# Order of loads and splits at the head of each layer's passes, and the second layer's first norm factors made in the output projection

## The chip, the cores and the metric

The kernel runs on one core of a Trainium2 chip. The metric is the device time of one execution in microseconds, the median of several runs. The engines named below are TensorE (PE; its weight loads PEld), VectorE (DVE), ScalarE (ACT), GpSimd (POOL) and SyncE (SP), which issues every DMA of this kernel. Each engine works through its own instructions in a fixed order.

## The reference: what is computed

Two layers over 2048 tokens of width 1024, in float32. Each layer normalises x, applies one input projection whose columns are split between two groups of heads, mixes them, and adds the output projection to x:

```
h = rmsnorm(x, norm_g[l]);  z = h @ w_in[l]
g_q, g_k, g_v, g_lr, g_gate, c_q, c_kv, k_pe, m_gate = split(z)
log_a = log_sigmoid(g_lr @ w_gla_gate_up[l] + b_gla_gate[l]) / 16
o_gla = gla_mix(g_q, g_k, g_v, log_a, gla_norm_g[l]) * silu(g_gate)    # chunked gated linear attention
q  = rmsnorm(rmsnorm(c_q) @ w_uq[l]);  k, v = from rmsnorm(c_kv) @ w_ukv[l] and k_pe
o_mla = block_causal_attention(rope(q), rope(k), v) * silu(m_gate)
x = x + concat([o_gla, o_mla]) @ w_out[l]
```

## The kernel before

Tokens are cut into 16 tiles of 128, taken in 8 pairs. To keep float32 accuracy every large product is three matmuls (`mm3`, L98 to L101): both operands are split into a rounded high part (made on ScalarE) and the rest (made on VectorE or GpSimd); high times high, high times low and low times high are summed. `block` (L321) runs such a product over the 8 slices of the width (k = 0 to 7) and, after a slice, calls what a dictionary `ins` holds for it. So "at k = 3" means: these instructions stand in TensorE's order behind slice 3, with four groups of three matmuls of the block done.

Each layer has four stages.

1. `pass1` (L364) computes for each pair of tiles (`pair`, L592) four kinds of block: `mi` (latents, rotary key, low-rank gate input) for tile a and b, then `qk` and `v` for a, then `qk` and `v` for b. x is not normalised ahead of the product; the factor 1/rms of each token is kept in `rt` and applied to the results. Between the slices stand the small steps of linear attention: `gates_a` transposes the low-rank input `lr` that `lat_chain` made with the factor, `gates_b` multiplies it by the gate weights (`lg`), `gates_c` sums the log gates (`bp`), `gla_kv` updates the state (`kv`), `gla_o` makes the output (`op`). `tail(t)` says at which k the last two come.
2. `pass2` (L711) multiplies by the two gate weights (`gt`, `mg`), applies SiLU (`gate_y`, `gate_m`), transposes the gated output tile `on` (`out_t`) and makes the queries from the latent (`queries`, with the weight `w_uq` split into `uq`). It runs in the same pairs.
3. `phase_b` is causal attention, head by head.
4. `phase_c` is the output projection: for each quarter q of the tokens 8 column blocks m, each a product `co` over 8 slices, then `done` adds x. After the first layer `done` also stores the new x (`xd`) and sums its squares over the columns (`ac`, stored as `sd[q]`).

Where the factors come from: in the first layer `norm_load(t)` loads a tile of x (`xn`, one buffer) and `norm_s(t)` squares and sums it on ScalarE, and for two tiles at a time `norm` makes the factors. In the second layer `load_s(q)` loads `sd[q]` (tile `ss`) and `norm_q(q)` sums it over the partitions by four matmuls with a column of ones (each recorded as two), then `norm`. The factors of the first four tiles are made at slice 2 of the very first `mi` block (L599).

The order of work: TensorE runs in program order throughout. In the first pair of each layer ScalarE and VectorE run in program order as well (`BOOT`, in the `with` at the end of `pass1`); there the loads and the splits of the weights are listed by hand, and `boot.update` places some of them by (block, k). Everywhere else, and for SP and GpSimd everywhere, a planner lays down each engine's order at build time from durations that it assumes, among ready instructions in program order. A tile's buffers are shared by tag: in `pass1` and `pass2` the tag "x" has three buffers of 1024 columns, "stg" three staging buffers that weights, `kq`, `vr`, `on`, `qs` and others take in turn. A load into a buffer waits until its last user is done.

The `w_uq` splits: `split_small` (L282) loads 128x384, ScalarE makes the high part and VectorE the low part; there are four of them, written at the start of `pass2.run`.

Of the kernel before, what the change touches and what calls it, by code (L numbers as in the profile page):

```python
# [9 lines left out]
F32 = mybir.dt.float32  # L10
# [3 lines left out]
ALU = mybir.AluOpType  # L14
# [5 lines left out]
P = 128  # L20
# [33 lines left out]
def trunk(ctx: ExitStack, tc: tile.TileContext, x, xT, xt, positions, w_mi, w_qk, w_v, w_gt, w_mg, pk, w3s,  # L54
# [306 lines left out]
        V.tensor_tensor(out=rt[:, t:t + n, 2], in0=r, in1=r, op=ALU.mult)  # L361


    def pass1(l, wp, pp, w1, lat, hT01):  # L364
        sm = smalls[l]

# [17 lines left out]

        def norm_load(t):

            sss[t] = w1.tile([P, D], F32, tag="xn", name="xn", bufs=1)
            dma(sss[t], x[t * P:(t + 1) * P, :])

        def norm_s(t):  # L390
# [9 lines left out]
            dma(sss[q], sd[q])  # L400

        def norm_q(q):
            ps, ss = pp.tile([P, 8], F32, tag="tp", name="tp"), sss.pop(q)
            for i in range(4):
                T.matmul(ps[:, 2 * i:2 * i + 2], lhsT=ss[:, i * P:(i + 1) * P], rhs=ones, start=True, stop=True)
            v = w1.tile([P, 4], F32, tag="xv", name="xv")
            V.tensor_scalar(out=v, in0=ps[:, 0:8:2], scalar1=1.0 / D, scalar2=None, op0=ALU.mult)
            norm(w1, v, 4 * q, 4)

        def lat_chain(t, mi):  # L410
            lt = lr[:, t % 2]
# [162 lines left out]
            dma(od[t], osn)  # L574

        def tail(t):
            return {2: [lambda: gla_kv(t)], 4: [lambda: gla_o(t)]}

        def go(f, *a):
            return lambda: f(*a)  # L580
# [11 lines left out]
        def pair(p):  # L592
            a, b = 2 * p, 2 * p + 1
            more = b + 1 < NT
            bt = [{k[1]: v for k, v in boot.items() if k[0] == i and p == 0} for i in range(4)]
            mi = acc(pp, "mi")
            block(mi, hTs[a], wi["mi"], 464,
                  merge(bt[0], tail(a - 1) if p else {}, {0: [go(prep_h, b, 0)], 2: [go(prep_h, b, 1)]} if p else {},
                        {2: [go(norm_q, 0)]} if l > 0 and p == 0 else {}))  # L599
            lat_chain(a, mi)  # L600
            if p == 0:
                sm["finish_w3"]()
                if l == 0:
                    A.activation(out=tri_r, in_=tri, func=AF.Copy)
            mi = acc(pp, "mi")
            if l > 0 and p % 2 == 1 and more:
                load_s(p // 2 + 1)
            block(mi, hTs[b], wi["mi"], 464, merge({3 if p else 5: [go(gates_a, a)], 5 if p else 7: [go(gates_b, a)]}, bt[1]))
            lat_chain(b, mi)
            if p == 1 and l == 0:  # L610
                tc.keep_in_program_order(V.tensor_copy(pos_f, pos_i))
            if p == 2 and l == 0:
                rotary(w1, gps(pp, [P, 512], "pps"))
            wl = {}
            if not more:

                for which, blks in (("gt", (2, 3)), ("mg", (4, 5))):
                    pc = wi_pieces(l, which, pool_stage(wp, 2)(512))
                    for i, (load, split) in enumerate(pc):
                        wl.setdefault(blks[i // 2], {})[2 + 4 * (i % 2)] = [load, split]  # L620
            qk = acc(pp, "qk")
            block(qk, hTs[a], wi["qk"], 512,
                  merge({1: [go(lat_t, a)], 4: [go(gates_c, a)], 5: [go(gates_a, b)]}, bt[2], wl.get(2, {}),
                        {0: [go(prep_x, b + 1)], 2: [go(norm_load, b + 1)] if l == 0 else []} if more else {}))
            gla_b(a, qk)
            vp = acc(pp, "vp")
            block(vp, hTs[a], wi["v"], 512,
                  merge({0: [go(gates_b, b)], 1: [go(lat_t, b)], 3: [go(gla_qT, a)], 6: [go(gla_at, a), go(gates_c, b)]}, bt[3],
                        wl.get(3, {})))
            gla_v(a, vp)  # L630
            qk = acc(pp, "qk")
            block(qk, hTs[b], wi["qk"], 512,
                  merge(tail(a), {0: [go(prep_x, b + 2)], 3: [go(norm_s, b + 1), go(norm_load, b + 2)] if l == 0 else [], 6: [go(prep_h, b + 1, 0)]} if more
                        else {0: [go(pass2.prep, l, wp, 0)]}, wl.get(4, {})))
            gla_b(b, qk)
            vp = acc(pp, "vp")
            block(vp, hTs[b], wi["v"], 512,
                  merge({3: [go(gla_qT, b)], 6: [go(gla_at, b)]},
                        {0: [go(prep_h, b + 1, 1)], 4: [go(norm_s, b + 2)] if l == 0 else [go(norm_q, p // 2 + 1)] if p % 2 else []} if more else {}, wl.get(5, {})))
            gla_v(b, vp)  # L640

        with tc.manual_schedule(engines=BOOT):
            if l == 0:
# [10 lines left out]
                for load, _ in pm[1:]:  # L654
                    load()
                prep_x(1)
                dma(cst[:, 0:C_MASK], consts[:, 0:C_MASK])
                layer_small(0)
                norm_load(0)
                for load, _ in pq:  # L660
                    load()
                dma(cst[:, C_MASK:C_KEPT], consts[:, C_MASK:C_KEPT])
# [7 lines left out]
                pm[2][1]()  # L670
                pm[3][1]()
                prep_h(1, 0)
                prep_h(1, 1)
                norm_s(0)
                norm_load(1)
                norm_s(1)
                pv[0][0]()
                boot.update({(0, 4): [pq[0][1]], (0, 6): [pq[1][1]], (1, 2): [pq[2][1]],
                             (1, 5): [pq[3][1], pv[1][0]], (2, 1): [pv[0][1], pv[2][0], pv[3][0]], (2, 4): [pv[1][1]],
                             (2, 7): [pv[2][1]], (3, 2): [pv[3][1]]})  # L680
            else:
                load_s(0)
                pv = wi_pieces(l, "v", pool_stage(wp, 2)(512))
                pv[0][0]()
                pv[1][0]()
# [11 lines left out]
    class pass2:  # L697
# [13 lines left out]
        def run(l, wp, pp, w2, gt0, lat):  # L711
# [14 lines left out]
            for b in range(NT // 4):  # L726
                ts_ = slice(4 * b, 4 * b + 4)
                rope(G, w2, kpe[:, ts_, :], kpe[:, ts_, :], 4, cos[:, ts_, :], sin[:, ts_, :], nsin[:, ts_, :],
                     "qr")
            uq = w2.tile([P, 2, 2, 768], F32R, name="uq", bufs=1)  # L730
            for k in range(2):
                for c in range(2):
                    cs = slice(c * 384, c * 384 + 384)
                    split_small(gens.ast, w_uq[l, k * P:(k + 1) * P, cs], 384, sm["mqg"][:, k:k + 1],
                                uq[:, 0, k, cs], uq[:, 1, k, cs])

            qlats = {}

# [69 lines left out]
            def at(p, blk, k, f):  # L808
                ins.setdefault((p, blk), {}).setdefault(k, []).append(f)

            for g, p in enumerate(PRE):
                at(p, 0, 2, go(gens.lat, 0, g))
                at(p, 0, 6, go(gens.kv, 0, g))
                pt = p if g < 2 else NT // 2 - 1
                at(pt, 2, 3 * (g % 2) + 1, go(gens.t, 0, g))
                at(pt, 2, 3 * (g % 2) + 2, go(gens.tr, 0, g))
# [357 lines left out]
    def phase_c(l, wc, pp, yu):  # L1174
# [9 lines left out]
        def prep_x(t):  # L1184
            xn[t] = wc.tile([P, D], F32, tag="x", name="xt", bufs=2)
            dma(xn[t], x_src(l + 1, t).rearrange("p k c -> p (k c)"))

        def prep_h(t, half):
            if half == 0:
                hT01[t] = hT_tile("hT")  # L1190
            split_x(xn[t], hT01[t], half)
# [52 lines left out]
        for q in range(NQD):  # L1244
# [10 lines left out]
            for m in range(KT):  # L1255
# [17 lines left out]
                if last and more:  # L1273
                    if m == 4:
                        ins.setdefault(0, []).append(lambda: load_wi(l + 1, "qk", wc))
                    for t in range(2):
                        if m == 3 + t:
                            ins.setdefault(3, []).append(go(prep_x, t))
                        if m == 5 + t:
                            ins.setdefault(2, []).append(go(prep_h, t, 0))  # L1280
                            ins.setdefault(3, []).append(go(prep_h, t, 1))
# [95 lines left out]
```

## Time and profile before

| | |
|---|---|
| median of 3 runs | 2327.22 us (2324.18 to 2328.4) |
| profiled execution | 2326.9 us, its span 2325.1 us |
| TensorE busy | 2250.5 us, 97% of the span |
| VectorE, ScalarE, GpSimd busy | 1441.2, 1326.5, 425.6 us |
| DMA | 204.78 MB, mean 88 GB/s |

The span is the time from the first to the last recorded instruction. A busy TensorE is not one at its peak: matmuls overlap, and their duration doubles when the granted clock is at half. The busy shares are means over stages with different limits, so the stages are read one by one, by what each engine waited for.

### The profile page before, as it was taken

To read this page: it belongs to the slowest core of one execution; us is meant where nothing else is said; L and a number is where in the kernel's file an instruction comes from. 1 tells how busy PE (TensorE), PEld (TensorE's weight loads), DVE (VectorE), ACT (ScalarE), POOL (GpSimd) and SP (SyncE) were. 2 spreads that over 40 slices of the span, in tenths; PEclk is the share of its full clock that TensorE was granted. 3 is DMA by queue.
4 is the path that set the end of the run, shared out by engine and by line. 5 is a ranking of instruction groups with operands and counts; after the bars stand their busy time and mean duration, and the time that the engine had idled before them with its cause. 6 is when DMAs were issued, how large, how long until landed. Compare 5 with 4: busy or idle time off the path is not lost.

```text
span 2325.1 us, 37191 instructions
## 1 busy us (share of the span) xinstructions
PE 2250.5 (97%) x12597; PEld 1938.4 (83%) x12597; DVE 1441.2 (62%) x4421; ACT 1326.5 (57%) x3624; POOL 425.6 (18%) x627
## 2 busy tenths in 40 slices
PE   5899999999999999999989999999999999999999
PEld 4778887788899998988878888878888999988887
DVE  4465556677788888743235555576768888875211
ACT  5554546677777777642234554567667777776100
POOL 0000001343322122233200000023333121123000
PEclk8899999999999999999999999999999999999999
DMA  5320113443311111165421110244433111112642
GB/s 179 110 72 32 42 39 131 129 136 113 108 41 47 36 43 47 47 211 187 146 91 46 42 41 33 69 132 131 138 95 101 34 48 39 40 54 81 196 133 82
DMA packets 168607, 204.78 MB, mean 88 GB/s; under 512 B 12560, under 2 KB 123232, under 8 KB 168416
## 3 DMA queue, kind: packets, MB, share of 16 engines
q1 hardware_dynamic: 168416, 202.40, 27.7%
q8 instruction: 100, 1.64, 0.3%
q14 instruction: 91, 0.75, 0.1%
HBM read 138.39 MB, written 63.96 MB: 87 GB/s over the span
## 4 chain that ended last, share of the span: by engine, by line
PE 84%; ACT 6%; DVE 4%; DMA 4%; issue 1%; POOL 1%; SPq 0%; ACTq 0%; DVEq 0%; POOLq 0%
PE tp L96 8%; PE co L99 5%; PE co L101 5%; PE co L100 5%; PE sp L985 3%; PE sp L982 3%; PE sp L986 3%; PE sp L984 2%; PE sp L983 2%; PE mg L101 2%; PE mg L99 2%; PE o L1057 2%; PE mg L100 2%; PE o L1056 2%; PE vp L99 2%; PE o L1055 2%
## 5 line engine op out<-in xcount | busy, mean ns | idle before, releaser
L100 PE MATMUL co<-y,wo_h 128*128 128x512 f32 x512 | 199.3, 389 | 0.0
L99 PE MATMUL co<-y,wo_h 128*128 128x512 f32 x512 | 199.3, 389 | 0.0
L101 PE MATMUL co<-y,wo_l 128*128 128x512 f32 x512 | 199.2, 389 | 0.0
L993 DVE TENSOR_SCALAR_CACHE_REDUCE p<-sp 128x512 f32<-128x512 f32 (+5 forms) x304 | 172.9, 573 | 22.2 <-PE sp L986 18.5
L1000 ACT ACTIVATE p<-p,nm 128x128 f32<-128x128 f32 (+15 forms) x128 | 153.8, 1202 | 36.4 <-DVE nm L999 31.3
L1035 ACT ACTIVATE ph<-tp 128x512 fp32r<-128x512 f32 x224 | 130.6, 594 | 75.9 <-PE tp L96 67.2
L1036 DVE TENSOR_TENSOR pl<-tp,ph 128x512 fp32r<-128x512 f32 x224 | 151.9, 686 | 34.0 <-ACT ph L1035 32.8
L1055 PE MATMUL o<-ph,v 128*128 128x256 f32 x576 | 168.1, 292 | 4.6 <-ACT ph L1035 2.6
L1221 DVE TENSOR_TENSOR xc<-co,xc 128x512 f32<-128x512 f32 x64 | 44.1, 690 | 206.2 <-PE co L101 195.2
L1057 PE MATMUL o<-pl,v 128*128 128x256 f32 x576 | 170.1, 295 | 1.8 <-DVE pl L1036 1.3
L96 PE MATMUL tp<-cst,p 128*128 128x128 f32 x1088 | 166.5, 275 | 1.3 <-ACT p L1000 1.0
L1056 PE MATMUL o<-ph,v 128*128 128x256 f32 x576 | 161.3, 280 | 0.0
L186 POOL TENSOR_TENSOR ropeu<-kpe,cos 128x256 f32<-128x256 f32 x8 | 7.0, 869 | 751.2 <-DVE Z L546 750.9
L982 PE MATMUL sp<-kn,q 128*128 128x512 f32 (+3 forms) x320 | 129.4, 405 | 6.0 <-ACT q L917 4.9
L96 PEld LDWEIGHTS tp<-cst,p 128*128 128x128 f32 x1088 | 125.0, 141 | 9.9 <-ACT p L1000 2.3
L1055 PEld LDWEIGHTS o<-ph,v 128*128 128x128 f32 x576 | 109.2, 190 | 11.9 <-ACT ph L1035 4.7
L983 PE MATMUL sp<-kn,q 128*128 128x512 f32 (+3 forms) x320 | 116.4, 364 | 0.0
L984 PE MATMUL sp<-kn,q 128*128 128x512 f32 (+3 forms) x320 | 116.3, 369 | 0.0
L985 PE MATMUL sp<-kr,q 128*128 128x512 f32 (+3 forms) x320 | 115.3, 367 | 0.9 <-ACT q L932 0.5
L1057 PEld LDWEIGHTS o<-pl,v 128*128 128x128 f32 x576 | 108.8, 189 | 7.2 <-DVE pl L1036 3.2
L986 PE MATMUL sp<-kr,q 128*128 128x512 f32 (+3 forms) x320 | 114.2, 367 | 0.0
L100 PEld LDWEIGHTS co<-y,wo_h 128*128 128x128 f32 x512 | 96.1, 188 | 20.2 <-POOL y L1163 0.3
(279 smaller groups left out, 6760.6 us busy)
## 6 DMA issues: line engine op xcount, KB each, us to landing
yst<-yd SPq DMA_DIRECT2D x28, 512.0 KB, 4.9
qd<-qs SPq DMA_DIRECT2D x32, 384.0 KB, 2.9
gst<-qd SPq DMA_DIRECT2D x64, 192.0 KB, 2.5
xn<-in_x SPq DMA_DIRECT2D x16, 512.0 KB, 3.3
od<-osn SPq DMA_DIRECT2D x32, 256.0 KB, 2.0
hf<-in_xt SPq DMA_DIRECT2D x16, 512.0 KB, 3.4
on<-od SPq DMA_DIRECT2D x32, 256.0 KB, 2.8
yd<-yT SPq DMA_DIRECT2D x32, 256.0 KB, 2.8
```

Source lines behind the costliest of these rows:

```text
L96: T.transpose(o, i, ident[:k, :k])
L99: T.matmul(o, lhsT=lh, rhs=rh, start=start, stop=False)
L100: T.matmul(o, lhsT=lh, rhs=rl, start=False, stop=False)
L101: T.matmul(o, lhsT=ll, rhs=rh, start=False, stop=stop)
L982: T.matmul(o, lhsT=qn[:, 0, ts_], rhs=kn[:, 0, k0:k1], start=True, stop=False)
L983: T.matmul(o, lhsT=qn[:, 0, ts_], rhs=kn[:, 1, k0:k1], start=False, stop=False)
L985: T.matmul(o, lhsT=qrr[:, 0, ts_], rhs=kr[:, c0:c1], start=False, stop=False)
L986: T.matmul(o, lhsT=qrr[:, 1, ts_], rhs=kr[:, c0:c1], start=False, stop=True)
L993: V.tensor_scalar(out=pt[:, c0:c0 + w], in0=sp[:, 0:w], scalar1=0.0, scalar2=-3e38, op0=ALU.add, op1=ALU.max, accum_out=mx[:, m:m + 1])
L1055: T.matmul(o[:, s], lhsT=vh, rhs=ph[:, j, s], start=(kb == 0), stop=False)
L1056: T.matmul(o[:, s], lhsT=vl, rhs=ph[:, j, s], start=False, stop=False)
L1057: T.matmul(o[:, s], lhsT=vh, rhs=pl[:, j, s], start=False, stop=(last and j == 1))
```

## The change

It has four parts.

- In the first layer's head both `norm_load(0)` and `norm_load(1)` are issued behind the second tile of x and ahead of the constants and the small weights; the second has a buffer of the tag "x" of its own. `norm_s(0)` and `norm_s(1)` stand between the two halves of the second tile's split.
- In every pair `gla_kv` and `gla_o` move from k = 2 and 4 to 3 and 5, `gates_b` of the first tile from 5 to 6 (not in the first pair), `gates_b` of the second from 0 to 1 and its `gates_c` from 6 to 7.
- In `pass2` the four `w_uq` splits are written into the first pair's second and third block at k = 1 and 5, no longer at its start.
- The factors of the second layer's tiles 0 to 3 are made in the output projection of the first: `norm0` loads `sd[0]` and makes the sums and factors, at slice 4 of column block 6 of the last quarter. `load_s(0)` and `norm_q(0)` at the start of the second layer go. `norm4` is the shared body.

```diff
--- before.py
+++ after.py
@@ -361,6 +361,14 @@
         V.tensor_tensor(out=rt[:, t:t + n, 2], in0=r, in1=r, op=ALU.mult)
 
 
+    def norm4(pool, ps, ss, q):
+        for i in range(4):
+            T.matmul(ps[:, 2 * i:2 * i + 2], lhsT=ss[:, i * P:(i + 1) * P], rhs=ones, start=True, stop=True)
+        v = pool.tile([P, 4], F32, tag="xv", name="xv")
+        V.tensor_scalar(out=v, in0=ps[:, 0:8:2], scalar1=1.0 / D, scalar2=None, op0=ALU.mult)
+        norm(pool, v, 4 * q, 4)
+
+
     def pass1(l, wp, pp, w1, lat, hT01):
         sm = smalls[l]
 
@@ -384,7 +392,7 @@
 
         def norm_load(t):
 
-            sss[t] = w1.tile([P, D], F32, tag="xn", name="xn", bufs=1)
+            sss[t] = x_tile(wp, "xn") if t == 1 else w1.tile([P, D], F32, tag="xn", name="xn", bufs=1)
             dma(sss[t], x[t * P:(t + 1) * P, :])
 
         def norm_s(t):
@@ -400,12 +408,7 @@
             dma(sss[q], sd[q])
 
         def norm_q(q):
-            ps, ss = pp.tile([P, 8], F32, tag="tp", name="tp"), sss.pop(q)
-            for i in range(4):
-                T.matmul(ps[:, 2 * i:2 * i + 2], lhsT=ss[:, i * P:(i + 1) * P], rhs=ones, start=True, stop=True)
-            v = w1.tile([P, 4], F32, tag="xv", name="xv")
-            V.tensor_scalar(out=v, in0=ps[:, 0:8:2], scalar1=1.0 / D, scalar2=None, op0=ALU.mult)
-            norm(w1, v, 4 * q, 4)
+            norm4(w1, pp.tile([P, 8], F32, tag="tp", name="tp"), sss.pop(q), q)
 
         def lat_chain(t, mi):
             lt = lr[:, t % 2]
@@ -574,7 +577,7 @@
             dma(od[t], osn)
 
         def tail(t):
-            return {2: [lambda: gla_kv(t)], 4: [lambda: gla_o(t)]}
+            return {3: [lambda: gla_kv(t)], 5: [lambda: gla_o(t)]}
 
         def go(f, *a):
             return lambda: f(*a)
@@ -596,7 +599,7 @@
             mi = acc(pp, "mi")
             block(mi, hTs[a], wi["mi"], 464,
                   merge(bt[0], tail(a - 1) if p else {}, {0: [go(prep_h, b, 0)], 2: [go(prep_h, b, 1)]} if p else {},
-                        {2: [go(norm_q, 0)]} if l > 0 and p == 0 else {}))
+                        {}))
             lat_chain(a, mi)
             if p == 0:
                 sm["finish_w3"]()
@@ -605,7 +608,7 @@
             mi = acc(pp, "mi")
             if l > 0 and p % 2 == 1 and more:
                 load_s(p // 2 + 1)
-            block(mi, hTs[b], wi["mi"], 464, merge({3 if p else 5: [go(gates_a, a)], 5 if p else 7: [go(gates_b, a)]}, bt[1]))
+            block(mi, hTs[b], wi["mi"], 464, merge({3 if p else 5: [go(gates_a, a)], 6 if p else 7: [go(gates_b, a)]}, bt[1]))
             lat_chain(b, mi)
             if p == 1 and l == 0:
                 tc.keep_in_program_order(V.tensor_copy(pos_f, pos_i))
@@ -625,7 +628,7 @@
             gla_b(a, qk)
             vp = acc(pp, "vp")
             block(vp, hTs[a], wi["v"], 512,
-                  merge({0: [go(gates_b, b)], 1: [go(lat_t, b)], 3: [go(gla_qT, a)], 6: [go(gla_at, a), go(gates_c, b)]}, bt[3],
+                  merge({1: [go(gates_b, b), go(lat_t, b)], 3: [go(gla_qT, a)], 6: [go(gla_at, a)], 7: [go(gates_c, b)]}, bt[3],
                         wl.get(3, {})))
             gla_v(a, vp)
             qk = acc(pp, "qk")
@@ -654,9 +657,10 @@
                 for load, _ in pm[1:]:
                     load()
                 prep_x(1)
+                norm_load(0)
+                norm_load(1)
                 dma(cst[:, 0:C_MASK], consts[:, 0:C_MASK])
                 layer_small(0)
-                norm_load(0)
                 for load, _ in pq:
                     load()
                 dma(cst[:, C_MASK:C_KEPT], consts[:, C_MASK:C_KEPT])
@@ -670,16 +674,14 @@
                 pm[2][1]()
                 pm[3][1]()
                 prep_h(1, 0)
+                norm_s(0)
+                norm_s(1)
                 prep_h(1, 1)
-                norm_s(0)
-                norm_load(1)
-                norm_s(1)
                 pv[0][0]()
                 boot.update({(0, 4): [pq[0][1]], (0, 6): [pq[1][1]], (1, 2): [pq[2][1]],
                              (1, 5): [pq[3][1], pv[1][0]], (2, 1): [pv[0][1], pv[2][0], pv[3][0]], (2, 4): [pv[1][1]],
                              (2, 7): [pv[2][1]], (3, 2): [pv[3][1]]})
             else:
-                load_s(0)
                 pv = wi_pieces(l, "v", pool_stage(wp, 2)(512))
                 pv[0][0]()
                 pv[1][0]()
@@ -728,11 +730,12 @@
                 rope(G, w2, kpe[:, ts_, :], kpe[:, ts_, :], 4, cos[:, ts_, :], sin[:, ts_, :], nsin[:, ts_, :],
                      "qr")
             uq = w2.tile([P, 2, 2, 768], F32R, name="uq", bufs=1)
+            uqs = []
             for k in range(2):
                 for c in range(2):
                     cs = slice(c * 384, c * 384 + 384)
-                    split_small(gens.ast, w_uq[l, k * P:(k + 1) * P, cs], 384, sm["mqg"][:, k:k + 1],
-                                uq[:, 0, k, cs], uq[:, 1, k, cs])
+                    uqs.append(go(split_small, gens.ast, w_uq[l, k * P:(k + 1) * P, cs], 384, sm["mqg"][:, k:k + 1],
+                                  uq[:, 0, k, cs], uq[:, 1, k, cs]))
 
             qlats = {}
 
@@ -808,6 +811,8 @@
             def at(p, blk, k, f):
                 ins.setdefault((p, blk), {}).setdefault(k, []).append(f)
 
+            for i, f in enumerate(uqs):
+                at(0, 1 + i // 2, 1 + 4 * (i % 2), f)
             for g, p in enumerate(PRE):
                 at(p, 0, 2, go(gens.lat, 0, g))
                 at(p, 0, 6, go(gens.kv, 0, g))
@@ -1185,6 +1190,11 @@
             xn[t] = wc.tile([P, D], F32, tag="x", name="xt", bufs=2)
             dma(xn[t], x_src(l + 1, t).rearrange("p k c -> p (k c)"))
 
+        def norm0():
+            ss = wc.tile([P, QD], F32, tag="xc", name="ss", bufs=4)
+            dma(ss, sd[0])
+            norm4(wc, acc(pp, "co"), ss, 0)
+
         def prep_h(t, half):
             if half == 0:
                 hT01[t] = hT_tile("hT")
@@ -1273,6 +1283,8 @@
                 if last and more:
                     if m == 4:
                         ins.setdefault(0, []).append(lambda: load_wi(l + 1, "qk", wc))
+                    if m == 6:
+                        ins.setdefault(4, []).append(norm0)
                     for t in range(2):
                         if m == 3 + t:
                             ins.setdefault(3, []).append(go(prep_x, t))
```

## Rows read from the trace of the kernel before

**Rows 1.** The page's line of busy time: us (share of the span) xinstructions, by engine

```profile
PE 2250.5 (97%) x12597; PEld 1938.4 (83%) x12597; DVE 1441.2 (62%) x4421; ACT 1326.5 (57%) x3624; POOL 425.6 (18%) x627
```

**Rows 2.** TensorE's waits, 0 to 420 us: total, times, longest

```profile
PE tp L96 <- DVE lr L415: 15.1, 1, 15.1
...
PE tp L96 <- DVE on L784: 3.4, 1, 3.4
...
PE lg L451 <- ACT lrT L446: 3.0, 2, 1.8
...
PE kv L100 <- DVE vr L533: 2.9, 4, 1.4
...
PE kv L99 <- ACT vr L532: 2.8, 3, 1.8
```

**Rows 3.** TensorE's waits, 1170 to 1560 us

```profile
PE tp L405 <- DMA ss<-sd: 4.4, 1, 4.4
...
PE tp L96 <- DVE on L784: 4.2, 1, 4.2
...
PE lg L451 <- ACT lrT L446: 2.5, 3, 1.2
```

**Rows 4.** Timeline of SP, 0 to 60 us: start, duration, engine, line, what

```profile
7.32 0.35 SPq L60 DMA_DIRECT2D xn<-in_x  x1
...
20.91 8.73 SPq L60 DMA_DIRECT2D xn<-in_x  x2
```

**Rows 5.** Timeline of ScalarE, 0 to 60 us (in brackets: idle before, releaser)

```profile
14.31 1.06 ACT L394 ACTIVATE xn<-xn 128x1024 f32<-128x1024 f32 x1 [0.95 <-DMA xn<-in_x]
...
28.14 1.06 ACT L394 ACTIVATE xn<-xn 128x1024 f32<-128x1024 f32 x1 [12.68 <-DMA xn<-in_x]
```

**Rows 6.** Timeline of VectorE, 0 to 60 us

```profile
12.87 1.29 DVE L352 TENSOR_TENSOR hT<-xt,hT 128x512 fp32r<-128x512 f32 x2
...
31.00 2.73 DVE L267 SCALAR_TENSOR_TENSOR wqk_l<-bootqk,pk,wqk_h 128x512 fp32r<-128x512 f32 x4
```

**Rows 7.** Timeline of TensorE, 0 to 60 us

```profile
18.75 0.37 PE L101 MATMUL mi<-wmi_h,hT 128*128 128x464 f32 x1
```

**Rows 8.** Three stretches: us, busy us by engine, granted clock, DMA share, GB/s

```profile
12.80:19.10 6.30, 6.30 (x30) 5.31 (x28) 1.36 (x3) 1.71 (x4) 0.00 (x0) 1.00 1.03 402
...
415.70:419.10 3.40, 3.38 (x10) 2.88 (x11) 0.47 (x1) 0.60 (x1) 0.00 (x0) 0.50 0.21 62
...
1187.67:1190.60 2.93, 2.93 (x8) 2.53 (x9) 1.29 (x9) 0.41 (x2) 0.00 (x0) 0.51 1.00 365
```

**Rows 9.** Timelines of SP, ScalarE, GpSimd and TensorE, around 406 to 421 us

```profile
406.63 0.33 SPq L60 DMA_DIRECT2D stg<-in_w_uq  x1
...
409.04 0.62 ACT L285 ACTIVATE uq<-stg,pk 128x384 fp32r<-128x384 f32 x1 [4.15 <-DMA stg<-in_w_uq]
...
409.45 0.75 POOL L191 TENSOR_TENSOR kpe<-ropeu,ropew 128x256 f32<-128x256 f32 x1
...
421.23 0.33 PE L99 MATMUL qp<-uq,lh 128*128 128x384 f32 x1
```

**Rows 10.** Instructions on the tile uq: duration ns min/median/max, first and last start

```profile
L285 ACT ACTIVATE uq<-stg,pk x8: 601/602/619, 403.3 to 1544.8; 128x384 fp32r<-128x384 f32 x8
...
L286 DVE SCALAR_TENSOR_TENSOR uq<-stg,pk,uq x8: 609/918/1098, 405.9 to 1545.6; 128x384 fp32r<-128x384 f32 x8
```

**Rows 11.** Timeline of SP, 1165 to 1240 us

```profile
1182.93 0.33 SPq L60 DMA_DIRECT2D sd<-ac  x1
...
1183.68 0.33 SPq L60 DMA_DIRECT2D ss<-sd  x1
...
1184.07 1.41 SPq L60 DMA_DIRECT2D stg<-in_w_v  x3
```

**Rows 12.** Timeline of TensorE, 1172 to 1215 us

```profile
1186.41 1.26 PE L405 MATMUL tp<-ones,ss 128*128 128x2 f32 x8 [4.42 <-DMA ss<-sd]
```

**Rows 13.** ScalarE's waits, 60 to 200 us: total, times, longest

```profile
ACT xn L394 <- DMA xn<-in_x: 15.8, 10, 3.3
```

## The prediction

> **What bounds the kernel now.** I read the page's busy line first: TensorE is busy 2250.5 of 2325.1 us [rows 1], so a change can give back only the 74.6 us in which it stands, and what low clock goes with them. The next view was what TensorE waited for, over the two stretches that the diff touches. In the first layer's passes four causes carry most of it: one wait of 15.1 us for the low-rank tile `lr`, one of 3.4 us for the gated tile `on`, 5.7 us for the value splits before `kv`, 3.0 us for the transposed gate factors before `lg` [rows 2]. In the second layer: 4.4 us for the load of the squared sums `ss`, 4.2 us for `on`, 2.5 us for `lg` [rows 3]. Then the timelines of SP, ScalarE and VectorE around each wait, to see what stands ahead of the awaited instruction on its own queue. I take the four parts in that order; what is saved goes to the end, since TensorE is the engine that is busy 97% of the span.
>
> **A. Head of the first layer.** Before: the first load of `xn` is issued at 7.32, the second only at 20.91, behind the value weights and two x tiles, because both share one buffer [rows 4]. ScalarE squares the second at 28.14 after 12.7 us of waiting [rows 5]. The factors are there at 31.0, where VectorE goes on with four splits of 2.73 us in all that stand ahead of `lr` by the hand order [rows 6]. TensorE ended its sixth step of the second tile at about 19.1 (18.75 and 0.37) [rows 7], and 15.1 us later [rows 2], at 34.2, it transposes `lr`.
> After: two buffers, both loads right behind the second x tile and ahead of three small transfers (about 0.2 MB). The first square now starts at 14.31, as soon as its load lands, 7.0 us after issue [rows 4, 5]; 0.2 MB less ahead of it at 402 GB/s [rows 8] is 0.5 us, so 13.8. The second load, 0.52 MB at that rate, lands 1.3 us later, at 15.1; its square takes 1.1 us, and from the end of the square to the factors it was 1.8 us (29.2 to 31.0) [rows 5, 6]: factors at 18.0. New ahead of `lr` is the second half of the second tile's split, 0.65 us (half of 1.29), then the same 2.73 us of weight splits [rows 6] and the 0.5 us from there to the transpose: 21.9. That is 12.3 us before 34.2. The later half split delays TensorE's fifth and sixth step by up to 1 us, inside the 2 to 3 us that it will still stand. The qk weights are queued behind 0.5 MB more, 1.3 us; the splits that need them start no earlier than 17.6 and find the first there. Bounds: 9 us, if the second load comes 3 us late in a full queue, and 13.3 us, if both are there when ScalarE is free. I take 12.
>
> The Trainium skill, DMA: Bandwidth & Descriptors, section Anatomy of one DMA, gives a transfer about 2 us and its bytes at 436 GB/s, so 3.2 us for this load. By that both would have landed before ScalarE is free and A would be about 1 us more. The trace's 7.0 us in this stretch [rows 4, 5] disagree, since other transfers are ahead.
>
> **B. Five steps moved by one k step in every pair.** `kv`, the output step `gla_o`, `lg` of the first tile, and `lg` and the cumulative sums of the second come one group of three matmuls later. Such a group takes 0.63 us at full clock (30 matmuls of 464 columns in 6.30 us, so 0.21 each [rows 8]), a little more where it has 512 columns. Nothing is added, and what feeds these steps runs on as before, so each wait shrinks by up to that. Eligible are four places of `kv` (5.7 us) and two of `lg` (3.0) in the first layer [rows 2], two of `lg` in the second (2.5, less a small third one that is not moved) [rows 3]: eight times 0.65 is 5.2 us. Bounds: nothing, where ScalarE's order changes with it, and all 10.9 us. I take 5.
>
> **C. The four splits of `w_uq` spread over two blocks.** Before, the fourth load is issued at 406.63, when a staging buffer comes free, and ScalarE, whose order is fixed, stands 4.15 us until 409.04 for it; the SiLU of both first gates is queued behind [rows 9]. That is what `on` comes late by: without this wait and the split of 0.6 us [rows 10] the chain ends 4.7 us sooner, more than the 3.4 us that TensorE stood. After the wait TensorE ran 3.4 us at a granted clock of 0.50 [rows 8], worth 1.7 us. So 5.1 in the first layer; 4.2 [rows 3] and by estimate again 1.7 in the second, 5.9; 11 in all. What is late next: the last `uq` split, wanted at 421.23 less 5, about 416 [rows 9]. Three staging buffers are shared with two `on` tiles, so the loads run one behind the other: about 2.4 us for a load [rows 9] and 0.6 and 0.9 for the two halves of a split [rows 10], some 4 us a round; two rounds after about 405 make 413, and one more round would make 417, a wait of 1 to 2 us. The rotary work on GpSimd, which goes on to 410 [rows 9], is not moved. Bounds: 3 us, if the wait reappears before the queries in both layers, and 11. I take 10.
>
> **D. Factors of the second layer's first four tiles.** Before: the load of `ss` stands on SP behind the store of the last `sd`, which goes at 1182.93; it is issued at 1183.68 [rows 11], and TensorE, in order, waits 4.4 us [rows 3] and spends 1.26 us on the eight short matmuls at 1186.41 [rows 12]. The next eight matmuls take 2.93 us at a granted clock of 0.51, which is 1.2 GHz, where eight times 0.21 would be 1.7 [rows 8]: 1.25 lost. Sum 6.9 us. After, the eight short matmuls stand in the last column block but one of the output projection; they cost at most the 1.26 again, I take 1.0. Net 5.9. Their load needs a buffer of the residual tiles that comes free one column block earlier, and it lands 2.7 us after issue [rows 11, 12] in a stretch where SP has little to do. The nine small VectorE and two ScalarE instructions lie in the idle time of both engines there. What is late next: the value weights, issued from 1184.07 on behind the same store [rows 11], and wanted now some 7 us earlier; the first should land at about 1187.5, when ScalarE reaches it, so I allow 0.5 us. Bounds: 3 and 7. I take 6.
>
> **Sum.** 12 + 5 + 10 + 6 = 33 us. The profiled execution took 2326.9 us (span 2325.1 and 1.8 around it), 0.3 below the median of 2327.2. 2326.9 - 33 is 2293.9: **2294 us**.
>
> **Rivals.**
> *The waits come back one step later (C and D).* The `uq` splits and the value weights are loaded one after the other through few buffers, and TensorE then stands at the queries and at `lg` of the second layer's first pair. For it: the serial rounds in C, the store ahead of the weights in D. Against: 3 to 4 us of slack in my count. C gives 3, D 3, B 3, A 12: 21 us, 2306 us.
> *The change doesn't do what it says in D.* The load of `ss` is written directly ahead of the matmuls that want it; if it is put on SP behind the store of the column block before, TensorE stands in the output projection, and at most D's 6 us go: 2300 us. Against: the trace has loads issued far ahead of their place in the program, as the third `xn`, which SP sends by 29.6 [rows 4] though it is written in the first pair's qk block.
> *Slower: squares of the rows ahead of urgent work on ScalarE.* From 60 to 200 us ScalarE stands 15.8 us, ten times, for `xn` loads through their single buffer [rows 13], and holds up what TensorE wants. The whole stretch now starts 12 us earlier. Fourteen tiles are squared after the first two, and if each waits a full 3.3 us (the longest now) and all of it reaches TensorE, that is 46 us, less what `kv` and `lg` of these pairs lose to it now, some 8: 38 lost against 33 won, 2332 us. It decides if more than some 40 us of those waits reach TensorE. Against: most of the 15.8 us now fall where TensorE has its own work.
>
> **Chances.** Forecast 0.68 (own range 2286 to 2304), waits come back 0.16, D undone 0.08, in between and about equal 0.04, slower 0.04. The range 2284 to 2312 takes in the rivals but the last: its low end is the sum of the upper bounds (13.3 + 10.9 + 11 + 7 is 42), its high end the lower bounds together (15). About 0.2%, 4.7 us, is what can be told from no change: faster 0.92, within it 0.04, slower 0.04.
>
> **What would show it.** A: the second `xn` load issued before 8, the transpose of `lr` at 21 to 24. B: waits for `kv` and `lg` shorter by 0.6 us each. C: no wait of TensorE for `on` above 1 us in either layer, and none before the first `qp`. D: no wait for `ss` at the start of the second layer, its eight short matmuls some 7 us before the end of the output projection, and ScalarE's splits of the value weights at about 1188. Wrong would be: a wait above 6 us left in the head, a new wait for `uq` or the value weights, or waits for `ln` in the first layer's early pairs that grow with the shift.

## The result, and the profile after

The changed kernel took 2283.66 us (median of 4 runs, 2282.41 to 2286.36) against 2326.9 for the kernel before beside it: ratio 0.9817, interval 0.980 to 0.9834; in a second measurement 2283.59 against 2326.01, ratio 0.9822 (0.9809 to 0.9836). That is 42 to 43 us faster. Forecast were 33 us, so 2294, in the range 2284 to 2312: the change went the way that was forecast and was worth some 30% more. The median lies at the very low end of that range, 0.3 us under 2284 before rounding, and below the forecast's own range of 2286 to 2304. The profiled execution took 2282.41 us, its span is 2280.6.

The page's busy line after, beside [rows 1]: TensorE lost 20.5 us of busy time with the same 12597 matmuls, so about half of the 44.5 us by which the span shrank is not idle time at all. The 74.6 us in which TensorE stood did not bound the gain: a matmul whose weights are loaded late, under a running matmul, is recorded as longer and counts as busy (`kv` below, a mean of 333 and of 283 ns).

```profile
PE 2230.0 (98%) x12597; PEld 1927.8 (85%) x12597; DVE 1443.4 (63%) x4421; ACT 1321.4 (58%) x3624; POOL 424.2 (19%) x627
```

Part of the busy time was low clock. Span and mean granted clock, before and after:

```profile
core 0: 2325.1 us, clock 0.987
```

```profile
core 0: 2280.6 us, clock 0.997
```

At two levels, 1.00 and 0.50, that is about 60 us at half before, some 11 of them inside the wait of 15.1 us for `lr`, which was granted 0.63, and 14 us after. By the price in [rows 8] (2.93 us at 0.51 for what takes 1.7 at full clock) this makes, as an estimate, 15 us of the 44.5, where the prediction's terms hold 4.65 (1.7, 1.7 and 1.25). Most of it lies in the head and in pairs 1 and 2, and it differs between executions (last section). The recorded duration of a matmul does not double at half clock: matmuls of 464 columns show 0.59 for 0.37 us, with 0.39 for 0.21 us between starts (kernel before, at 36 and at 18 us).

TensorE's waits after, 0 to 420 us (engine, line, releaser: total, times, longest), beside [rows 2]: `lr` 15.1 to 2.0, `kv` 5.7 to 3.4, `lg` for `lrT` 3.0 to 1.0, `on` from 3.4 to 0.2. New in the list is `bp`; `at` rose from 0.2 to 1.3 and `qkp` from 0.5 to 1.6. `ln`, which the prediction did not count, fell from 3.6 to 1.4. First that line before, then the list after.

```profile
PE tp L96 <- DVE ln L429: 3.6, 2, 2.3
```

```profile
PE tp L96 <- DVE lr L418: 2.0, 1, 2.0
PE kv L100 <- DVE vr L536: 1.8, 2, 1.4
...
PE kv L99 <- ACT vr L535: 1.6, 1, 1.6
PE bp L465 <- ACT lah L457: 1.5, 1, 1.5
PE tp L96 <- DVE ln L432: 1.4, 1, 1.4
PE at L524 <- ACT qkT L510: 1.3, 3, 0.6
PE lg L454 <- ACT lrT L449: 1.0, 2, 0.7
...
PE tp L96 <- DVE on L787: 0.2, 1, 0.2
```

The same from 1120 to 1575 us, beside [rows 3]: `ss` is gone, `on` fell from 4.2 to 0.4, `lg` from 2.5 to 1.3; a wait for the low part of `uq` and one of the first `mi` for a residual add (`xc`) are new.

```profile
PE qp L100 <- DVE uq L286: 1.6, 1, 1.6
PE lg L454 <- ACT lrT L449: 1.3, 3, 0.7
PE tp L96 <- DVE qkp L482: 1.2, 1, 1.2
PE mi L99 <- DVE xc L1231: 0.8, 1, 0.8
...
PE tp L96 <- DVE on L787: 0.4, 1, 0.4
```

Where it came from can be read without any list of waits. Both kernels issue the same matmuls, so the start of one block's first matmul before, less its start in another kernel, is what that kernel has won up to there; the differences of that by stretch, from one profiled execution each (us won against the kernel before, negative is lost):

```
stretch                       changed   A    B    C    D   B+C  no kv no gates no B  best2
head and first pair              15.5 12.4 -0.5  0.5  1.4  1.3   14.2   15.1   12.4   15.2
pairs 1 and 2                     7.1  0.2  6.4  0.6  1.2  5.9    7.0    4.7    0.1    6.0
pairs 3 to 7                      3.2  0.1  3.3  0.1  0.1  3.3    1.3    2.6    0.1    3.3
pass 2, first pair                5.5  1.4 -0.6  5.9  1.4  5.7    5.4    4.9    5.7    5.7
to last quarter of projection    -0.6 -0.5 -0.1 -0.6 -0.1 -1.3   -1.6   -1.3   -1.7   -0.6
last quarter                     -1.9  0.0  0.0  0.0 -1.9  0.0   -1.9   -1.9   -1.9   -1.0
first block of layer 2            7.0 -0.3 -0.8 -1.3  7.0  0.0    7.0    7.0    7.0    7.1
rest of its pass 1                4.4  0.0  3.8  0.0  0.2  3.7    0.4    3.1    0.1    4.3
its pass 2, first pair            5.0  0.0 -0.6  6.1  0.3  5.7    4.3    3.7    4.9    6.8
rest                             -0.7  1.4 -0.8  1.1  0.2 -0.8    0.2    0.5    0.4   -0.1
whole span                       44.5 14.7 10.1 12.4  9.8 23.6   36.3   38.3   27.1   46.8
```

The columns after the first are the experiments below. A second execution of the changed kernel gave 12.1 in the first row and the same within 0.5 in the rows of pass 1 and pass 2; what that is, stands at the end. Rows that a part does not touch differ from nothing by up to 1.4 us (D alone: 1.4, 1.2 and 1.4 in three of the first four rows), but by 0.1 at most in pairs 3 to 7 and by 0.2 in the rest of layer 2's pass 1.

### The profile page after: what moved, and what is told of

It is laid out like the page before. It is cut to its first block, busy times and chain, and to the rows that moved or that the text cites. A ratio compares the mean times of both kernels' runs of the same rounds, so it can differ in the third digit from the quotient of the medians.

```text
span 2280.6 us, 37201 instructions
## 1 busy us (share of the span) xinstructions
PE 2230.0 (98%) x12597; PEld 1927.8 (85%) x12597; DVE 1443.4 (63%) x4421; ACT 1321.4 (58%) x3624; POOL 424.2 (19%) x627
## 3 DMA queue, kind: packets, MB, share of 16 engines
q8 instruction: 100, 1.64, 0.3%
## 4 chain that ended last, share of the span: by engine, by line
PE 86%; ACT 5%; DVE 4%; DMA 3%; issue 1%; POOL 1%; SPq 0%; ACTq 0%; POOLq 0%; DVEq 0%
PE tp L96 8%; PE co L101 5%; PE co L99 5%; PE co L100 5%; PE sp L987 3%; PE sp L990 3%; PE sp L991 3%; PE gt L101 3%; PE gt L100 3%; PE gt L99 3%; PE sp L988 2%; PE o L1062 2%; PE sp L989 2%; PE o L1061 2%; PE mg L101 2%; PE mg L99 2%
## 5 line engine op out<-in xcount | busy, mean ns | idle before, releaser
L998 DVE TENSOR_SCALAR_CACHE_REDUCE p<-sp 128x512 f32<-128x512 f32 (+5 forms) x304 | 173.2, 574 | 21.9 <-PE sp L991 18.0
```

What stands on the lines that cost most here:

```text
L998: V.tensor_scalar(out=pt[:, c0:c0 + w], in0=sp[:, 0:w], scalar1=0.0, scalar2=-3e38, op0=ALU.add, op1=ALU.max, accum_out=mx[:, m:m + 1])
```

## The experiments

**The parts one by one.** Each is the kernel before with one part of the diff.

```diff
 A: -  prep_h(1, 1); norm_s(0); norm_load(1); norm_s(1)
    +  norm_load(0); norm_load(1)   # behind prep_x(1)
    +  norm_s(0); norm_s(1); prep_h(1, 1)
 B: -  {2: [lambda: gla_kv(t)], 4: [lambda: gla_o(t)]}     # and the gate steps
    +  {3: [lambda: gla_kv(t)], 5: [lambda: gla_o(t)]}
 C: +  at(0, 1 + i // 2, 1 + 4 * (i % 2), f)
 D: +  if m == 6: ins.setdefault(4, []).append(norm0)
```

A. 

> The changed kernel gained 44 us where 33 were forecast; by the starts of equal TensorE blocks, 13 us of it are there at the transpose of `lr`, 15.5 at tile 2, and 7 more come in pairs 1 and 2. Theory 1 (the moved steps were worth far more than their listed waits): the new load order alone gives 13 to 16 us, and pairs 1 and 2 of the first layer keep their old waits for `kv`, `lg` and `ln`. Theory 2 (the earlier start also takes those waits away, by where the `xn` squares fall on ScalarE): 20 to 23 us, with the extra 7 already visible in pairs 1 and 2.

B. 

> Theory 1: moving the five steps by one k step is worth 13 to 17 us alone: some 5 to 7 in pairs 1 and 2 of the first layer, 3 in pairs 3 to 7, 4.4 in the second layer, mostly from waits of 0.2 to 0.3 us of the second `kv` matmul that the list of waits leaves out. Theory 2: 8 us, with pairs 1 and 2 nearly as before.

C. 

> Spreading the four weight splits alone: 10 to 11 us by both theories, about 5 in each layer at the transposes of the first gated tile, and a wait of 0 to 2 us for the last low part before the queries.

D. 

> Factors in the output projection alone: 5 us (7 won at the second layer's first block; 1 paid for the eight short matmuls, 0.8 for a new wait of the first block of the second layer for VectorE's last addition, since its accumulator now falls on that bank). If that wait is not of this part it is absent here, and the gain is 6.

Measured beside 2324.55 us for the kernel before: A 2311.91 (ratio 0.9945, 0.9928 to 0.9961), 12.6 us; B 2315.64 (0.9964, 0.9951 to 0.9977), 8.9; C 2315.33 (0.9962, 0.9947 to 0.9977), 9.2; D 2317.94 (0.9972, 0.9961 to 0.9983), 6.6. A, C and D are near their forecasts (A a little under the 13 to 16 us of theory 1; D at the 6 us of no wait, though the wait of 0.8 us for the last addition is there in its trace). With A alone pairs 1 and 2 are unchanged (0.2): the theory that the earlier start takes their waits away falls, and so does the fear that it makes them worse. B alone is nearly twice its forecast of 5 (interval 5.3 to 11.4 us). Of its two theories the first had the places right (6.4, 3.3 and 3.8 us in the rows of pass 1) and the sum wrong: 13 to 17 us were expected and 8.9 measured, the second theory's number. The four sum to 37.3, 5 us less than the whole.

**B with C.** B alone waits longer for `on` (4.1 and 4.9 us, where it was 3.4 and 4.2): TensorE comes there sooner, and ScalarE still stands 4.19 us for the last `uq` load. That was to be the missing 5 us.

```diff
 kernel before with B and C:
+  return {3: [lambda: gla_kv(t)], 5: [lambda: gla_o(t)]}
+  at(0, 1 + i // 2, 1 + 4 * (i % 2), f)
```

> Kernel before with parts B (five steps one slice later) and C (the four splits of w_uq spread) alone; their single runs gave 8.9 and 9.2 us. Theory: B's gain is partly swallowed at the wait for the gated tile on, whose end is set by the load of uq and not by TensorE, as long as C is not there; so B and C together give 23 to 25 us less than before, and the gain at the second pair of pass 2 of each layer lies 5 us or more above the sum of the two single ledgers there. Rival: the parts add up, 18 us, and what the whole change has beyond the sum of its parts comes from another pair of them.

2301.31 against 2323.43, ratio 0.9905 (0.9891 to 0.9918): 22.1 us, below the theory's band and above the rival's 18; its interval, 19 to 25 us, takes in part of the band, so the table has to decide. In the two stretches where `on` is awaited it wins 5.7 and 5.7 us; the single kernels sum to 5.3 and 5.5 there. So the give-back is real (0.6 us in each of them with B alone), but it is not the missing 5 us, and that theory falls.

**The halves of B.** The changed kernel with one half put back:

```diff
 without the kv half:
-  return {3: [lambda: gla_kv(t)], 5: [lambda: gla_o(t)]}
+  return {2: [lambda: gla_kv(t)], 4: [lambda: gla_o(t)]}
 without the gate half:
-  {1: [go(gates_b, b), go(lat_t, b)], 3: [go(gla_qT, a)], 6: [go(gla_at, a)], 7: [go(gates_c, b)]}
+  {0: [go(gates_b, b)], 1: [go(lat_t, b)], 3: [go(gla_qT, a)], 6: [go(gla_at, a), go(gates_c, b)]}
```

> Changed kernel with gla_kv and gla_o left at k = 2 and 4; all else as changed. Theory: the short waits before kv (11.2 us in all 32 places before, 4.4 after) are nearly all that this move takes away: about 7 us slower than the changed kernel, some 2291. Rival: the move of the gate steps carries B, and this kernel is within 2 us of the changed one.

> Changed kernel with gates_b and gates_c left where they stood before; all else as changed. Theory: the remaining part of B, 5 to 7 us slower than the changed kernel, 2289 to 2291, with waits for lg of 2 to 3 us back in each first pass. Rival: the move of kv carries B, and this kernel is within 2 us of the changed one.

2291.1 us (2287.35 to 2297.51) and 2289.61 (2288.58 to 2290.91), ratios 0.9863 (0.9846 to 0.9881) and 0.9854 (0.9841 to 0.9868): 7.5 and 6.0 us above the changed kernel's 2283.6 of the other measurements, and 9.5 and 7.4 by the ratios to the kernel before beside each; the theory had about 7 and 5 to 7. Either way both halves count, and both rivals (within 2 us) fall. The table says where: the gate half alone (column "no kv") wins all of pairs 1 and 2 (7.0), the kv half (column "no gates") most of the undisturbed pairs (2.6 of 3.2, and 3.1 of 4.4 in the second layer).

**Without B, beside the changed kernel.**

```diff
 changed kernel, B put back:
-  return {3: [lambda: gla_kv(t)], 5: [lambda: gla_o(t)]}     # and the gate steps
+  return {2: [lambda: gla_kv(t)], 4: [lambda: gla_o(t)]}
```

> The changed kernel once more, so that the three others stand beside it on one chip. Expected: a ratio to the kernel before of 0.980 to 0.9834, as in its first runs.

> Changed kernel with all five steps of part B left where they stood before: parts A, C and D. Leaving out the kv half alone or the gate half alone left 36.3 and 38.3 us of the 44.5 us of the span. Theory (the parts add up): B is worth in here what it is worth alone, 9 to 11 us, so 2292 to 2294 and a span gain of about 34 us. Rival (the two halves only work together with the other parts): 15 us or more, 2298 or above.

2299.18 (2298.39 to 2299.78; ratio 0.9887, 0.9874 to 0.9901) beside 2283.59: B is worth 15.6 us in here, the rival's number, and A, C and D together are 26.8, forecast 28. So the whole excess over the forecast is B's, measured beside the other three parts.

What B takes away shows in this pair. TensorE's groups over pairs 3 to 7 (line, operation, shapes, count | busy us, mean ns | idle before), without B:

```profile
L100 PE MATMUL kv<-vr,kq 128*128 128x256 f32 x20 | 6.7, 333 | 0.3
...
L465 PE MATMUL bp<-lah,tri_r 128*128 128x256 f32 x20 | 4.5, 306 | 0.0
L454 PE MATMUL lg<-w3r,lrT 96*128 96x256 f32 x10 | 2.9, 294 | 1.2 <-ACT lrT L449 1.2
```

and in the changed kernel:

```profile
L100 PE MATMUL kv<-vr,kq 128*128 128x256 f32 x20 | 5.7, 283 | 0.0
...
L465 PE MATMUL bp<-lah,tri_r 128*128 128x256 f32 x20 | 4.0, 279 | 0.0
L454 PE MATMUL lg<-w3r,lrT 96*128 96x256 f32 x10 | 2.9, 294 | 0.7 <-ACT lrT L449 0.7
```

Only 0.8 us (0.3 for `kv`, 0.5 for `lg`) of the 3.1 won there is in these columns of idle time. A `kv` step is two groups of three matmuls; the first group of one in such a pair in the timeline of TensorE (start, duration), without B:

```profile
211.72 0.28 PE L99 MATMUL kv<-vr,kq 128*128 128x256 f32 x1
212.06 0.39 PE L100 MATMUL kv<-vr,kq 128*128 128x256 f32 x1
212.29 0.28 PE L101 MATMUL kv<-vr,kq 128*128 128x256 f32 x1
```

and the changed kernel:

```profile
201.69 0.28 PE L99 MATMUL kv<-vr,kq 128*128 128x256 f32 x1
201.81 0.28 PE L100 MATMUL kv<-vr,kq 128*128 128x256 f32 x1
201.93 0.28 PE L101 MATMUL kv<-vr,kq 128*128 128x256 f32 x1
```

From the first start to the third it takes 0.57 us and then 0.24. The second matmul wants the low part `vr` of VectorE, which ends at 212.01 there, and came 0.2 us late; no bracket marks that, and the list of waits of the matmuls (engine PE) leaves it out. The list of the weight loads (PEld) has it: the load of that matmul's weights stood 0.37 us for `vr`, under the running matmul. The rows are that load and VectorE's instruction, without B; then what that list of the kernel before holds for pairs 3 to 7 and for the second layer's pass 1 behind its first block:

```profile
212.06 0.19 PEld L100 LDWEIGHTS kv<-vr,kq 128*128 128x128 f32 x1 [0.37 <-DVE vr L536]
...
211.32 0.69 DVE L536 TENSOR_TENSOR vr<-vs,vr 128x512 fp32r<-128x512 f32 x1 [1.45 <-ACT vr L535]
```

```profile
PEld kv L100 <- DVE vr L533: 2.9, 10, 0.4
...
PEld kv L100 <- DVE vr L533: 4.3, 15, 0.4
```

In the changed kernel neither stretch has a line for `kv` in that list. Summed over all starts of matmuls, the matmuls of `kv` behind the first of each step give 2.4 us of the 3.1 in pairs 3 to 7 and 3.6 of the 4.3 in the second layer: 0.24 us for each of 25 steps, the 10 and 15 of these two lines. In pairs 1 and 2 it is mostly waits that the matmuls' list shows too; by the distances between starts `ln` gives 3.0, `lg` 2.5, `kv` 2.4, less 3.1 that `bp` and `at` wait longer; and 2.2 us in which the large matmuls run closer together, with a higher granted clock in these two pairs. That last part is not shown to be B's: a second execution of the changed kernel was granted 0.96 there and has 1.3 us of it, and D alone, without B, was granted 0.97. The three rows are that stretch without B, in the changed kernel and in its second execution (us, busy by engine, granted clock, DMA share, GB/s):

```profile
64.59:167.42 102.83, 91.24 (x463) 74.71 (x461) 58.10 (x224) 59.18 (x182) 0.00 (x0) 0.95 0.29 97
```

```profile
61.47:157.27 95.80, 87.94 (x462) 72.45 (x461) 58.94 (x224) 59.08 (x182) 0.00 (x0) 0.98 0.32 105
```

```profile
64.89:160.18 95.29, 89.12 (x462) 73.72 (x461) 59.21 (x224) 59.23 (x182) 0.00 (x0) 0.96 0.32 105
```

**Two new waits of the changed kernel, removed.** In the second layer the first `mi` stands for the last residual add, and `qp` for the low part of `uq`. TensorE, then VectorE ahead of that `qp`:

```profile
1151.10 0.47 PE L99 MATMUL mi<-wmi_h,hT 128*128 128x464 f32 x1 [0.78 <-DVE xc L1231]
...
1516.29 0.45 PE L100 MATMUL qp<-uq,lh 128*128 128x384 f32 x1 [1.64 <-DVE uq L286]
```

```profile
1513.76 1.48 DVE L709 TENSOR_TENSOR hT<-hf,hT 128x1024 fp32r<-128x1024 f32 x1
1515.16 1.07 DVE L286 SCALAR_TENSOR_TENSOR uq<-stg,pk,uq 128x384 fp32r<-128x384 f32 x1
```

A split of the third tile of x, 1.48 us, is laid ahead of the awaited one. Three kernels:

```diff
 bank (changed kernel, and):
-  norm4(wc, acc(pp, "co"), ss, 0)
+  norm4(wc, pp.tile([P, 8], F32, tag="ns", name="ns"), ss, 0)
 best (bank, and):
-  norm_s(0); norm_s(1); prep_h(1, 1)
+  norm_s(0); prep_h(1, 1); norm_s(1)
-  at(p, 3, 0, go(pass2.prep, l, wp, b + 1))
+  at(p, 3, 0 if p else 4, go(pass2.prep, l, wp, b + 1))
 best2 (bank, and):
-  at(p, b, 2, go(queries, t))
+  at(p, b, 2 if t else 5, go(queries, t))
```

> Changed kernel with one edit: the sums of norm0 are in a PSUM tile of a tag of its own, not in an accumulator of the ring that the output projection and the next layer's blocks take in turn. Theory (the extra tile shifts the ring, so the second layer's first mi block must wait until the last residual add has freed its bank): the wait of 0.78 us on that add goes, and the start of the second layer's first block comes 0.8 to 0.95 us sooner against the last co matmul; in the median 1 us, below what can be told. Rival: the residual add is what the next block waits for in any case, and the wait stays.

> Changed kernel with three edits: the sums of norm0 have an accumulator bank of their own (takes away the wait of 0.78 us of the second layer's first mi block for a bank that the last residual add frees), the second half of the second tile's split stands ahead of the second square (0.5 us of hT wait in the head), the first pair's query preparation stands at k = 4 of its block and not at 0 (1.64 us of wait for uq in the second layer). Theory: 0.8 + 0.5 + 1.6 = 2.9 us, less what falls elsewhere: 2281, 2 to 3 us faster than the changed kernel. Rival: TensorE meets the same work one wait later and it is within 1 us of the changed kernel.

> As the kernel with its own bank, and the queries of tile 0 moved from k = 2 to k = 5 of their block in pass 2, so that the last low part of uq (1.6 us late in the second layer) has 2 us more. Theory: 0.9 + 1.6 = 2.5 us faster than the changed kernel. Rival: the planner lays the low part of uq behind other work that is then due earlier, or the later queries hold a bank that the next block wants, and it is within 1 us.

Bank: 2283.93 us (2279.75 to 2285.6), ratio 0.9819 (0.9806 to 0.9832), no change in the median, but in the trace the wait for `xc` is gone and the last quarter loses 1.0 instead of 1.9. Best: 2282.78 (2282.02 to 2283.44), ratio 0.9825 (0.9812 to 0.9839), no gain that shows: its first edit brings the transpose of `lr` to 20.33 from 21.11, but by the third tile this is lost among what executions differ by (last section), and its last one did not change the order of VectorE, the wait for `uq` stayed at 1.6. Only the bank's part worked. Best2: 2280.46 (2278.34 to 2282.78), ratio 0.9807 (0.9794 to 0.982), 3.1 us faster than the changed kernel beside it with no run in common; by the table pass 2 of the second layer wins 6.8 for 5.0. Its list of waits for 1120 to 1575 us has neither `xc` nor `uq` any more. It is the fastest version tried.

## Why the prediction was right, and where its size was off

**A, forecast 12, measured 12.6.** The two loads go out together at 4.81, and the factors are there at 17.4 (forecast 18.0), the half split, the weight splits and then `lr` follow as counted, and `lr` is transposed at 21.11 (forecast 21.9, before 34.2). So the mechanism is the one forecast. SP, ScalarE and TensorE after, beside [rows 4, 5]:

```profile
4.81 1.28 SPq L60 DMA_DIRECT2D xn<-in_x  x2
```

```profile
12.87 1.06 ACT L402 ACTIVATE xn<-xn 128x1024 f32<-128x1024 f32 x1 [0.66 <-DMA xn<-in_x]
...
14.42 1.06 ACT L402 ACTIVATE xn<-xn 128x1024 f32<-128x1024 f32 x1 [0.40 <-DMA xn<-in_x]
```

```profile
18.03 0.48 PE L101 MATMUL mi<-wmi_h,hT 128*128 128x464 f32 x1 [0.50 <-DVE hT L352]
...
21.11 0.32 PE L96 MATMUL tp<-cst,lr 128*96 128x128 f32 x1 [1.97 <-DVE lr L418]
```

ScalarE still waited 0.66 and 0.40 us for the two loads, and took up the first 8.1 us after its issue, where 7.0 were taken. The Trainium skill, DMA: Bandwidth & Descriptors, section Anatomy of one DMA, fits about 2 us and the bytes at 436 GB/s to one transfer that GpSimd issues; by that an estimate for such a load is 3.2 us. These loads go by SP, with others ahead of them, so the fit was not made for them, and the trace has 8.1 us. The half split costs TensorE 0.50 us (forecast: up to 1, hidden in the wait for `lr`).

One term A put at nothing without saying so: the clock behind the wait. Before, TensorE was granted 0.50 for the 9.3 us behind the transpose; the rows are the wait and this stretch (us, busy by engine, granted clock, DMA share, GB/s):

```profile
19.10:34.20 15.10, 0.03 (x1) 0.00 (x0) 4.16 (x14) 4.01 (x8) 0.00 (x0) 0.63 0.65 244
34.20:43.50 9.30, 7.58 (x20) 5.79 (x21) 6.35 (x18) 6.68 (x21) 0.00 (x0) 0.50 0.04 12
```

After, there is low clock in the head too, of a length that differs by execution: 13.1 us won at the transpose became 15.5 at the third tile in the first execution of the changed kernel, 12.6 became 12.1 in the second, and with A alone 12.4 stayed 12.4. That this term came out near nothing there, and A at its forecast, is luck.

**B, forecast 5, measured 8.9 alone and 15.6 in the whole.** This is the step that was mis-sized. The forecast took "four places of `kv`" and "two of `lg`", 11.2 us of waits in the lists, and 0.65 us for each of eight. Those same rows did shrink by 5.5 us (11.2 to 5.7), so the mechanism (each wait shrinks as its step comes later) was right, and the count for what it counted. But three things are in no row that it took: some 0.24 us in each of 25 `kv` steps (6.0 us), which the list of the weight loads shows and that of the matmuls does not; the waits for `ln`, whose transposes stand right behind the moved `lg` (3.0 us in pairs 1 and 2, 0.8 and 1.0 elsewhere), of which 3.6 us stood in the list before and were not counted; and the 2.2 us by which the large matmuls run closer, which need not be B's. Against them `bp` and `at` wait longer. Over the three stretches of pass 1 that makes 14.4 us (7.0, 3.1 and 4.3). Even the upper bound of 10.9 was too low, since it was the sum of the same rows. That the forecast of the whole still held, at its edge, is owed to a range that had room for all upper bounds at once. Alone B wins 13.5 us in these stretches and gives 1.2 back at `on`; that its median is then only 8.9 (by the interval 5.3 to 11.4) I can't fully account for: 2.2 us are lost in stretches in which no step of B stands, and 1.2 are the profiled executions against the medians. Of the 6.7 us that B is worth more beside the other parts than alone, only 0.9 lie in pass 1 and 1.2 at `on`; the cause of the rest stays open.

**C, forecast 10, measured 9.2 alone, 10.5 by the table** (5.5 and 5.0). Both waits for `on` are gone, and the granted clock behind the first of them was 1.00 over 3.4 us where [rows 8] has 0.50:

```profile
386.00:389.40 3.40, 3.40 (x17) 2.88 (x18) 2.57 (x5) 2.50 (x4) 0.00 (x0) 1.00 0.47 137
```

In the second layer the "one more round" came true: 1.64 us at `qp`, inside the 1 to 2 us that were given for it. It is 0.5 and 0.6 us with C alone and with B and C, and 1.6 or 1.7 in all kernels with A and D too but best2; why those two add to it was not tried.

**D, forecast 6, measured 6.6 alone, 5.1 by the table.** The load of `ss` goes out at 1136.44, 5.3 us ahead of its matmuls:

```profile
1141.72 0.95 PE L366 MATMUL co<-ones,ss 128*128 128x2 f32 x8
```

The start of layer 2 won 7.0 (forecast 6.9). The eight short matmuls cost 0.95, as taken. What the forecast missed is a wait of 0.78: the sums take an accumulator out of the ring of four, so that the next layer's first block falls on the one that the last residual add must empty; with a bank of its own it is gone. The value weights are split from 1159.1 on, in step with the shift, and no wait for them is listed.

**The rivals.** The waits that come back are 1.6 and 0.8 us, not 12. The load of `ss` is not behind the store. The squares of the rows behind an earlier start cost nothing: A alone has pairs 1 and 2 as before within 0.2 us, and its wait for `ln` is the 3.6 us of the kernel before. The 6.9 us that TensorE still stands at its very first matmul, for the first weights, were 7.3 before and belong to no part.

## What to carry to other kernels

TensorE has two lists of waits, one for its matmuls and one for its weight loads, and a short wait of a weight load under a running matmul stands only in the second: here 25 waits of 0.4 us at most, 7.2 us in all, of which 6.0 were won. A step that recurs dozens of times can lose 0.2 us each time without a mark in the matmuls' list or in the idle column. Read both lists, and to price what they show compare, for each kind of small step, the start-to-start times of its matmuls with the fastest ones in the same trace, times the count; the bound for moving a step later is that sum, with the steps that stand right behind it, and not the sum of the matmuls' listed waits. A tile taken out of a rotating ring moves every later user by one place: give a one-off its own buffer, or count who comes to stand behind whom.

## What was not expected of the hardware

The head differs between executions of one kernel by its granted clock. In the 20 us from 40 us on TensorE was granted 1.00 in one execution of the changed kernel, in which it issued 85 matmuls, and 0.83 in a second one, in which it issued 74; up to the third tile the second lost 3.4 us against the first (15.5 and 12.1 won). The two rows:

```profile
40.00:60.00 20.00, 16.60 (x85) 12.54 (x83) 9.89 (x27) 9.96 (x28) 0.00 (x0) 1.00 0.11 39
```

```profile
40.00:60.00 20.00, 17.12 (x74) 13.18 (x72) 7.20 (x20) 8.46 (x25) 0.00 (x0) 0.83 0.08 26
```

Other kernels show 0.83, 0.91 or 1.00 there, and what the head wins goes with it: 12.1 to 13.4 us in the four executions with A's order of loads that were granted 0.83 (the second of the changed kernel, A alone, without B, best), 14.2 in the one with 0.91 (without the kv half), 15.1 to 15.6 in the four with 1.00. So differences of up to 3 us in the first row of the table are not the work of an edit, and the median over several runs is needed for A.
